# Adding x between two layers: accumulating transfers in place of loads and GpSimd adds

## The chip, the cores and the metric

The kernel runs on one core of one Trainium2 chip. The metric is the device time of one execution in microseconds (us). Three executions of the kernel before took 1881.49, 1882.27 and 1885.61 us, so the median is 1882.27 us. A further execution was profiled; all rows below are from it.

## The reference

A two-layer encoder trunk in float32, for 16 meta tokens, 512 prompt frames and 32 sample frames (560 columns in all), each with 2048 features:

```
def layer_forward(x, ...):
    u = rms_norm(x, pre_g)
    proj = einsum('btd,dc->btc', u, w_in)       # 2048 -> 6144 columns
    ...                                          # RG-LRU branch ya, attention branch yb
    y = einsum('btc,cd->btd', concatenate([ya, yb], -1), w_out)
    x = x + rms_norm(y, post_g)                  # <- the step that the change is about
    return x, ...
for l in range(2): x = layer_forward(x, ...)
```

The addition `x + rms_norm(y, post_g)` stands twice: between the layers, where the sum feeds layer 1 (`g_post` in the kernel), and at the end, where it is the output (`g_last`).

## The kernel before

Everything is held with features on the 128 partitions and the 560 columns along the free axis, so each activation is 16 feature tiles of 128x560. Weights and activations are float32, split into a high and a low part (`whi`, `wlo`; `uhi`, `ulo`); a product is three TensorE matmuls of 280 columns (`mm3`, L293 on, the matmul is L301): high x high, low activation x high weight, high activation x low weight. Weights come in chunks of 256 KB, four 128x128 blocks: SyncE loads `raw` (four buffers, L251), ScalarE rounds it to `whi` (L271) up to three chunks ahead of use (`w_ahead`), VectorE subtracts to get `wlo` (L281).

`R` holds 16 tiles of 128x560: first the mixed branches, then the rows of `y`. x itself does not fit in SBUF beside them; it lies in DRAM (`XD`).

Order is written by hand. All work beside the matmul stream is in Python generators that the class `Side` steps: after every two `mm3` (six matmuls, one tick) up to two generators that are due advance by one step, and `yield n` puts the next step n ticks on. Every engine takes its own instructions in this order, and waits for data that is not there.

Around the change: the last six output tiles of layer 0's W_out are computed for columns 0 to 279 (half 0), then again for columns 280 to 559 (half 1), each tile from four chunks. After each output tile `ev_y` scales it out of PSUM into `R` (VectorE, L1193), squares it (ScalarE, L1196) and sums the squares in `xcp` (GpSimd, L1200). At the end of half 0 the generator `0post0` is started (`side.add`, L1243), so it runs beside half 1's matmuls; `0post1` waits for it and runs beside layer 1's first products (`rows`, L1129), which for each feature tile k first ask that `ulo[k]` has been issued (`st["ready"]`).

One `g_post` (L991) makes the reciprocal root of the mean square (`rstd_half`, 128x280 matmul with ones at L428, Ln and Exp on ScalarE, four VectorE steps), then runs 19 steps. Step s multiplies `R[s]` by it (VectorE, L1015), adds x (GpSimd, L1016) from a buffer that a ScalarE-queued transfer filled one step earlier (L1001); two steps later ScalarE rounds the sum times the gain to `uhi` (L1020), stores the new x to DRAM (L1021) and squares it (L350); VectorE on every fourth tile, GpSimd on the others, adds the squares in the tile `accx` (L353, named e in the profile); one step later VectorE makes `ulo` (L1025). The pauses after the steps are 2, 2 and 4 ticks in turn (`RP`).

Of the kernel before, what the change touches and what calls it, by code (L numbers as in the profile page):

```python
# [10 lines left out]
F32 = mybir.dt.float32  # L11
F32R = mybir.dt.float32r
ACTF = mybir.ActivationFunctionType
ALU = mybir.AluOpType
# [13 lines left out]
T = META + SEQ + DEC  # L28
S0 = META + SEQ
KT = 16  # L30
# [7 lines left out]
WRAW, WSP = 4, 4  # L38

NB = 6  # L40
RP = (2, 2, 4)

KEPT = (("KH1", "KH2"), ("KL", "Q1"), ("Q2", "xch"), ("xcl", "Vh"), ("Vl", "MS"), ("PTh",), ("PTl",))
DQ, DS, DL = 7, 8, 9
# [1 line left out]
LY = 9  # L46
LF = 7
XR = 1
KF = 6
KRD, KPD, VRD, QPD = 6, 3, 2, 1  # L50
LS, L1, HL = 9, 1, 3
# [59 lines left out]
def hymba_step(ctx, tc, ins, onehot, outs):  # L111
    nc = tc.nc
    side = Side()
    st = {"of": [], "c": [0], "s": [0, 0], "c_i": 0, "s_i": 0}
# [11 lines left out]
    big = ctx.enter_context(tc.tile_pool(name="big", bufs=1))  # L126
# [3 lines left out]
    dram = ctx.enter_context(tc.tile_pool(name="dram", bufs=1, space=DRAM))  # L130
# [24 lines left out]

    uhi = [big.tile([128, T], F32R, name=f"uhi{k}") for k in range(KT)]
    ulo = [big.tile([128, T], F32R, name=f"ulo{k}") for k in range(KT)]
    R = [big.tile([128, T], F32, name=f"R{k}") for k in range(KT)]
    rstd = big.tile([128, T], F32, name="rstd")
    XD = [dram.tile([128, T], F32, name=f"xd{k}") for k in range(KT)]  # L160

    act_set(NLE)
    ident = const.tile([128, 128], F32, name="ident")
# [14 lines left out]
    def load_x(c):  # L178
        for i in range(4):
            nc.sync.dma_start(out=R[4 * c + i][:, 0:512],  # L180
                              in_=ins["x_prompt"][0, 128 * i:128 * i + 128, 512 * c:512 * c + 512])
# [37 lines left out]
    for l in range(DEPTH):  # L219
# [8 lines left out]
        for m in range(2, KT - NB):  # L228
            chunks += col_chunks(w_out, m)
            k = m - 3  # L230
# [130 lines left out]
    def x_squares(n):  # L361
# [3 lines left out]
        acc = ssq[:, 4 * i + c:4 * i + c + 1]  # L365
        x = R[min(4 * c + i, 15)][:, 0:512]
        if i < 4 and i % 2:
# [8 lines left out]
    def x_first(k):  # L376
# [5 lines left out]
        for i in range(4):  # L382
            p, at = (pa, META + 128 * i) if i < 2 else (pb, 128 * i - 256)
            nc.tensor.transpose(p[:, at:at + 128], R[4 * c + i][:, cs] if k else x0[:, i, :], ident)
        nc.tensor.transpose(pa[:, 0:META], v[DEC:DEC + META, ms], ident[DEC:DEC + META, DEC:DEC + META])
# [182 lines left out]
    def k_end(l, h):  # L568
# [4 lines left out]
        nc.gpsimd.tensor_copy(out=KS[:, PAST:PAST + DEC], in_=kT[:, S0:T])  # L573
        cK = R[8 + h][:, 0:512].rearrange("p (j c) -> p j c", j=4)
        cV = tmp.tile([128, 4, 128], F32, tag="cV", name="cV")
# [134 lines left out]
    def g_att(l, h, c0):  # L710
# [4 lines left out]
        PTs = tmp.tile([128, 5, 32], F32, tag="PTs", name="PTs")  # L715
        ot = R[8 + h]
        sq = wide("sq")
# [268 lines left out]
    def x_buffers():  # L986
        a, b = wide("i"), wide("r")
        c, d = (tmp.tile([128, n], F32, tag=t, name="xr") for t, n in (("KS", PAST + DEC), ("cV", 512)))
        return [a[:, 0:288], c, b[:, 0:288], d, a[:, 288:576], BM[:, 64:528], b[:, 288:576]]

    def g_post(l, half, ssy, ry):  # L991
        lo, hi = halves(l)[half]
        cs = slice(lo, hi)
        if not half:
            st["xr"] = x_buffers()
        xr = {}

        def load(k):
            if k < KT:
                xr[k] = st["xr"][k % 7][:, 0:hi - lo]  # L1000
                nc.scalar.dma_start(out=xr[k], in_=XD[k][:, cs])  # L1001

        while half and f"{l}post0" not in side.done:
            yield 1
        for k in range(XR):
            load(k)
        yield from grab("s", 5)
        rstd_half(ssy, ry, lo, hi, D)
        yield 2
        for s in range(KT + 3):  # L1010
            k = s
            if k < KT:
                r = R[k]
                load(k + XR)
                nc.vector.tensor_tensor(out=r[:, cs], in0=r[:, cs], in1=ry[:, cs], op=ALU.mult)  # L1015
                nc.gpsimd.tensor_tensor(out=r[:, cs], in0=r[:, cs], in1=xr[k], op=ALU.add)  # L1016
            k = s - 2
            if 0 <= k < KT:
                r = R[k]
                nc.scalar.activation(out=uhi[k][:, cs], in_=r[:, cs], func=ACTF.Copy, scale=col(l + 1, "pre", k))  # L1020
                nc.scalar.dma_start(out=XD[k][:, cs], in_=r[:, cs])  # L1021
                add_square(k, r[:, cs], lo, hi)
            k = s - 3
            if 0 <= k:
                nc.vector.scalar_tensor_tensor(out=ulo[k][:, cs], in0=R[k][:, cs], scalar=col(l + 1, "pre", k),  # L1025
                                               in1=uhi[k][:, cs].bitcast(F32), op0=ALU.mult, op1=ALU.subtract)
                st["ready"][half] = k + 1
            yield RP[s % len(RP)]
        yield from grab("s", 5)
        rstd_half([st["accx"][:, lo:hi]], rstd, lo, hi, D)  # L1030

# [3 lines left out]
    def x_late(k):  # L1035
# [3 lines left out]
        late[k] = late["t"][:, 288 * (k % 2):288 * (k % 2) + 288]  # L1039
        nc.sync.dma_start(out=late[k], in_=XD[k][:, 272:T])  # L1040

    def g_last(l, half, ssy, ry):
# [10 lines left out]

        for k in range(XR):
            load(k)
# [4 lines left out]
        for k in range(KT + 1 + lag):  # L1060
            if k < KT:
                load(k + XR)
                nc.vector.tensor_tensor(out=R[k][:, cs], in0=R[k][:, cs], in1=ry[:, cs], op=ALU.mult)  # L1063
# [25 lines left out]
    for l in range(DEPTH):  # L1089
# [38 lines left out]
        else:  # L1128
            def rows(half, acc, parts):  # L1129

                n = min(KF, len(KEPT))
                for part, ks in [(p, range(n)) for p in parts] + [(sum(parts, ()), range(n, KT))]:
# [25 lines left out]
        for kind, h in sched[l]:  # L1158
# [4 lines left out]
            for kc in range(4):  # L1163
                w = w_use()
                for kk in range(4):
                    k = 4 * kc + kk
# [17 lines left out]
        accy, ry = wide("xcp"), wide("sq")  # L1184
# [18 lines left out]
        for kc in range(8):  # L1203
            w = w_use()
            for kk in range(2):
                k = KT // 2 + 2 * kc + kk
# [84 lines left out]
```

## Time and profile before

| what | value |
|---|---|
| median of three executions | 1882.27 us (1881.49 to 1885.61) |
| the profiled execution | 1886.89 us |
| span of its instructions | 1885.2 us |
| TensorE matmul busy | 1843.5 us, 98% |
| VectorE busy | 1162.9 us, 62% |
| ScalarE busy | 909.5 us, 48% |
| GpSimd busy | 578.9 us, 31% |
| DMA, mean | 108 GB/s |

The engines are PE (TensorE matmuls), PEld (its weight loads), DVE (VectorE), ACT (ScalarE), POOL (GpSimd) and SP (SyncE); a name with q behind it is the engine's queue issuing a transfer. The half-0 tail of layer 0 ends at about 904.6 us of the span, half 1's matmuls run to about 951.6 us, and layer 1's first products from there to about 1007 us. A share of busy time over the whole span says little here: the place to read is the stretch from 904.6 to 1020 us.

### The profile page before, as it was taken

To read this page: it belongs to the slowest core of one execution; us is meant where nothing else is said; L and a number is where in the kernel's file an instruction comes from. 1 tells how busy PE (TensorE), PEld (TensorE's weight loads), DVE (VectorE), ACT (ScalarE), POOL (GpSimd) and SP (SyncE) were. 2 spreads that over 40 slices of the span, in tenths; PEclk is the share of its full clock that TensorE was granted. 3 is DMA by queue.
4 is the path that set the end of the run, shared out by engine and by line. 5 is a ranking of instruction groups with operands and counts; after the bars stand their busy time and mean duration, and the time that the engine had idled before them with its cause. 6 is when DMAs were issued, how large, how long until landed. Compare 5 with 4: busy or idle time off the path is not lost.

```text
span 1885.2 us, 37347 instructions
## 1 busy us (share of the span) xinstructions
PE 1843.5 (98%) x14196; PEld 1798.9 (95%) x14196; DVE 1162.9 (62%) x2484; ACT 909.5 (48%) x1831; POOL 578.9 (31%) x976
## 2 busy tenths in 40 slices
PE   7999999999999999999899999999999999999996
PEld 6999999999999999999888999999999999999995
DVE  6866656665666556434797776566565655563466
ACT  4555445454545536223555655453544544542343
POOL 3534232323323232011466242332423322211134
PEclk9999999999999999999999999999999999999998
DMA  7423232423333232335665232333323233233464
GB/s 232 130 77 105 76 104 65 110 75 109 83 89 99 74 111 71 99 100 142 197 196 150 60 111 75 107 94 87 107 76 108 64 110 100 78 93 115 125 192 140
DMA packets 334084, 204.35 MB, mean 108 GB/s; under 512 B 21100, under 2 KB 322612, under 8 KB 333904
## 3 DMA queue, kind: packets, MB, share of 16 engines
q1 hardware_dynamic: 311216, 164.44, 30.4%
q0 software_dynamic: 11168, 26.25, 5.0%
q10 hardware_dynamic: 11520, 11.28, 2.1%
q8 instruction: 111, 1.82, 0.4%
q14 instruction: 69, 0.57, 0.1%
HBM read 179.01 MB, written 22.89 MB: 107 GB/s over the span
## 4 chain that ended last, share of the span: by engine, by line
PE 87%; DVE 5%; issue 2%; POOL 2%; DMA 2%; ACT 1%; SPq 0%; ACTq 0%; DVEq 0%; POOLq 0%
PE pm L301 75%; PE sc L703 2%; PE sp L708 2%; DVE wlo L281 2%; PE sc L914 1%; PE sp L770 1%; PE sc L796 1%; PE sp L841 1%; PE sp L614 1%; DVE R L1063 1%; DMA raw<-in_w_in 1%; DMA R<-in_x_prompt 1%; DVE R L1015 0%; PE sc L301 0%; POOL R L1067 0%
## 5 line engine op out<-in xcount | busy, mean ns | idle before, releaser
L301 PE MATMUL pm<-uhi,whi 128*128 128x280 f32 (+3 forms) x3990 | 1181.9, 296 | 4.7 <-ACT whi L271 2.8
L301 PE MATMUL pm<-uhi,wlo 128*128 128x280 f32 (+3 forms) x3990 | 1160.5, 291 | 6.9 <-DVE wlo L281 6.8
L301 PE MATMUL pm<-ulo,whi 128*128 128x280 f32 (+3 forms) x3990 | 1158.8, 290 | 0.3 <-DVE ulo L395 0.3
L301 PEld LDWEIGHTS pm<-uhi,whi 128*128 128x128 f32 x3990 | 751.9, 188 | 18.1 <-issue 6.6
L301 PEld LDWEIGHTS pm<-uhi,wlo 128*128 128x128 f32 x3990 | 750.9, 188 | 10.7 <-DVE wlo L281 10.5
L301 PEld LDWEIGHTS pm<-ulo,whi 128*128 128x128 f32 x3990 | 752.2, 189 | 0.7 <-DVE ulo L395 0.6
L281 DVE TENSOR_TENSOR wlo<-raw,whi 128x512 fp32r<-128x512 f32 (+1 forms) x554 | 425.2, 774 | 264.5 <-ACT whi L271 261.2
L271 ACT CAST whi<-raw 128x512 fp32r<-128x512 f32 (+1 forms) x566 | 343.2, 614 | 388.8 <-PE pm L301 274.2
L689 ACT ACTIVATE e<-e,mx 128x144 f32<-128x144 f32 (+4 forms) x80 | 48.9, 611 | 165.5 <-DVE mx L686 165.5
L1200 POOL TENSOR_TENSOR xcp<-xcp,s 128x280 f32<-128x280 f32 (+2 forms) x56 | 43.1, 783 | 278.5 <-ACT s L1196 278.4
L140 ACT ACT_TABLE_LOAD x85 | 109.1, 1283 | 2.2 <-PEq L1273 0.8
L968 POOL TENSOR_TENSOR R<-R,z 128x280 f32<-128x280 f32 (+1 forms) x64 | 59.6, 954 | 147.1 <-DVE z L561 147.1
L761 POOL CAST PTm<-PTm 16x128 fp32r<-16x128 f32 (+1 forms) x72 | 22.0, 306 | 260.5 <-ACT PTm L756 260.2
L1196 ACT ACTIVATE s<-pm 128x280 f32<-128x280 f32 (+2 forms) x60 | 24.1, 402 | 125.3 <-DVE R L1193 124.6
L686 DVE CUSTOM_DVE_ANT_0 e<-sc,BM 128x144 f32<-128x144 f32 (+1 forms) x64 | 32.4, 507 | 57.6 <-PE sc L703 52.0
L844 DVE COPY R<-sp 128x288 f32<-128x288 f32 x16 | 7.3, 458 | 90.7 <-ACT sq L843 90.7
L1193 DVE TENSOR_SCALAR R<-pm,gvec 128x280 f32<-128x280 f32 (+2 forms) x64 | 30.2, 500 | 49.4 <-PE pm L301 49.4
L860 POOL TENSOR_TENSOR sq<-sq,s 128x560 f32<-128x560 f32 (+1 forms) x16 | 24.8, 1547 | 100.0 <-DVE s L444 96.2
L646 POOL COPY kv<-kv 128x16 f32<-128x16 f32 x15 | 3.0, 199 | 156.9 <-DVE kv L561 156.9
L703 PE MATMUL sc<-KH,Q 128*128 128x264 f32 (+4 forms) x176 | 45.2, 280 | 0.9 <-DVE mx L686 0.9
L703 PE MATMUL sc<-KL,Q 128*128 128x264 f32 (+4 forms) x176 | 45.3, 284 | 0.3 <-DVE KL L604 0.3
L689 ACT ACTIVATE s<-s,mx 128x144 f32<-128x144 f32 (+1 forms) x64 | 36.2, 565 | 19.6 <-DVE mx L686 17.8
(341 smaller groups left out, 2374.0 us busy)
## 6 DMA issues: line engine op xcount, KB each, us to landing
raw<-in_w_in SPq DMA_DIRECT2D x356, 256.0 KB, 2.9
raw<-in_w_out SPq DMA_DIRECT2D x176, 256.0 KB, 2.9
raw<-in_w_in SPq DMA_DIRECT2D x25, 192.0 KB, 3.3
xd<-R ACTq DMA_DIRECT2D x32, 140.0 KB, 2.8
R<-in_x_prompt SPq DMA_DIRECT2D x16, 256.0 KB, 5.2
R<-in_cache_k POOLq DMA_DIRECT2D x16, 256.0 KB, 4.9
cV<-in_cache_v POOLq DMA_DIRECT2D x16, 256.0 KB, 5.6
out_k_prompt<-s POOLq DMA_DIRECT2D x16, 256.0 KB, 5.2
```

The costliest lines, as they stand in the source:

```text
L140: nc.scalar.preload_act_table_set(name)
L271: nc.scalar.copy(out=hi[:, 0:n, :], in_=t[:, 0:n, :])
L281: q.tensor_tensor(out=lo[:, 0:n, :], in0=t[:, 0:n, :], in1=hi[:, 0:n, :].bitcast(F32), op=ALU.subtract)
L301: nc.tensor.matmul(out=ps[:, 0:n], lhsT=wt[:, blk, :], rhs=x[:, lo:hi], start=k == 0 and j == 0, stop=k == KT - 1 and j == 2)
L686: nc.vector.tensor_tensor_reduce(out=o2, in0=ps, in1=b2, scale=1.0, scalar=3.0e38, op0=ALU.add, op1=ALU.min, accum_out=m[0:rows, 0:1])
L689: nc.scalar.activation(out=o, in_=o, func=ACTF.Exp, scale=-1.0, bias=m[0:rows, 0:1], accum_out=m[0:rows, 1:2])
L703: nc.tensor.matmul(out=out, lhsT=st["Q"][m][:, qs], rhs=st[x][m][:, ks], start=x == "KH", stop=x == "KL")
L708: nc.tensor.matmul(out=out, lhsT=v[a], rhs=p[b], start=first and j == 0, stop=last and j == 2)
L860: nc.gpsimd.tensor_tensor(out=sq[:, c0:T], in0=sq[:, c0:T], in1=t[:, c0:T], op=ALU.mult)
L968: nc.gpsimd.tensor_tensor(out=r[:, lo:hi], in0=r[:, lo:hi], in1=z[:, lo:hi], op=ALU.mult)
L1193: nc.vector.tensor_scalar(out=R[m][:, cs], in0=ps[:, 0:hi - lo], scalar1=col(l, "post", m), scalar2=None, op0=ALU.mult)
L1200: nc.gpsimd.tensor_tensor(out=accy[:, cs], in0=accy[:, cs], in1=sq, op=ALU.add)
```

## The change

Between the layers x is added by the DMA engines. `R` and the DRAM copy of x become one tensor each (`RA`, `XA`), whose slices keep the old names, so that one transfer can span four feature tiles. After each fourth multiplication GpSimd issues one transfer that reads 128x4x280 values of x from DRAM and adds them into `RA` (`accum_op`). The loads into `xr` and the GpSimd additions of `g_post` are gone; `g_last` keeps its own. Steps now come every tick: multiplication s at step s, the transfer for tiles s-3 to s at s = 3, 7, 11, 15, `uhi` of tile k at step 12 + 2k, `ulo` at 14 + 2k; 45 steps in all.

```
+XB, XS, XL = 12, 2, 2
...
-    R = [big.tile([128, T], F32, name=f"R{k}") for k in range(KT)]
+    RA = big.tile([128, KT, T], F32, name="RA")
+    R = [RA[:, k, :] for k in range(KT)]
...
-    XD = [dram.tile([128, T], F32, name=f"xd{k}") for k in range(KT)]
+    XA = dram.tile([128, KT, T], F32, name="xa")
+    XD = [XA[:, k, :] for k in range(KT)]
...
-        for k in range(XR):
-            load(k)
         yield from grab("s", 5)
         rstd_half(ssy, ry, lo, hi, D)
         yield 2
-        for s in range(KT + 3):
-            k = s
-            if k < KT:
-                r = R[k]
-                load(k + XR)
-                nc.vector.tensor_tensor(out=r[:, cs], in0=r[:, cs], in1=ry[:, cs], op=ALU.mult)
-                nc.gpsimd.tensor_tensor(out=r[:, cs], in0=r[:, cs], in1=xr[k], op=ALU.add)
-            k = s - 2
-            if 0 <= k < KT:
+        for s in range(XB + XS * (KT - 1) + XL + 1):
+
+            if s < KT:
+                nc.vector.tensor_tensor(out=R[s][:, cs], in0=R[s][:, cs], in1=ry[:, cs], op=ALU.mult)
+                if s % 4 == 3:
+                    nc.gpsimd.dma_start(out=RA[:, s - 3:s + 1, cs], in_=XA[:, s - 3:s + 1, cs], accum_op=ALU.add)
+            k, o = divmod(s - XB, XS)
+            if 0 <= k < KT and o == 0:
                 r = R[k]
                 nc.scalar.activation(out=uhi[k][:, cs], in_=r[:, cs], func=ACTF.Copy, scale=col(l + 1, "pre", k))
                 nc.scalar.dma_start(out=XD[k][:, cs], in_=r[:, cs])
                 add_square(k, r[:, cs], lo, hi)
-            k = s - 3
-            if 0 <= k:
+            k, o = divmod(s - XB - XL, XS)
+            if 0 <= k < KT and o == 0:
                 nc.vector.scalar_tensor_tensor(out=ulo[k][:, cs], in0=R[k][:, cs], ...)
                 st["ready"][half] = k + 1
-            yield RP[s % len(RP)]
+            yield 1
```

GpSimd's queue where `0post0` starts, before (R_115 on are tiles 0 on of `R`; i, xr, r and BM are buffers of x; e is `accx`):

```order
L1016 TENSOR_TENSOR R_115<-R_115,i 128x280
L1200 TENSOR_TENSOR xcp<-xcp,s 128x280
L1016 TENSOR_TENSOR R_116<-R_116,xr 128x280
L1016 TENSOR_TENSOR R_117<-R_117,r 128x280
L1016 TENSOR_TENSOR R_118<-R_118,xr 128x280
L353 TENSOR_TENSOR e_9667<-e_9667,s 128x280
L1200 TENSOR_TENSOR xcp<-xcp,s 128x280
L1016 TENSOR_TENSOR R_119<-R_119,i 128x280
L353 TENSOR_TENSOR e_9667<-e_9667,s 128x280
L1016 TENSOR_TENSOR R_120<-R_120,BM 128x280
L1016 TENSOR_TENSOR R_121<-R_121,r 128x280
L353 TENSOR_TENSOR e_9667<-e_9667,s 128x280
```

The same place of GpSimd's queue now:

```order
L1007 DMA RA<-xa 128x4x280 x2
L1191 TENSOR_TENSOR xcp<-xcp,s 128x280
L1007 DMA RA<-xa 128x4x280
L356 TENSOR_TENSOR e_9637<-e_9637,s 128x280
L1007 DMA RA<-xa 128x4x280
L356 TENSOR_TENSOR e_9637<-e_9637,s 128x280
L1191 TENSOR_TENSOR xcp<-xcp,s 128x280
L356 TENSOR_TENSOR e_9637<-e_9637,s 128x280 x3
L1191 TENSOR_TENSOR xcp<-xcp,s 128x280
L356 TENSOR_TENSOR e_9637<-e_9637,s 128x280 x3
```

The additions of x have left the queue; four transfers stand in it, and the additions of squares stand closer together. ScalarE's queue up to the first `uhi` of half 0, before:

```order
L437 ACTIVATE sq<-sp,eps_t 128x280
L438 ACTIVATE sq<-sq 128x280
L271 CAST whi<-raw 128x512
L1001 DMA xr<-xd_133 128x280
L1196 ACTIVATE s<-pm 128x280
L271 CAST whi<-raw 128x512
L1001 DMA r<-xd_134 128x280
L271 CAST whi<-raw 128x512
L1001 DMA xr<-xd_135 128x280
L1020 ACTIVATE uhi_83<-R_115,gvec 128x280
L1021 DMA xd_132<-R_115 128x280
L350 ACTIVATE e_9667<-R_115 128x280
```

and now:

```order
L440 ACTIVATE sq<-sp,eps_t 128x280
L441 ACTIVATE sq<-sq 128x280
L274 CAST whi<-raw 128x512
L1187 ACTIVATE s<-pm 128x280
L274 CAST whi<-raw 128x512 x4
L1187 ACTIVATE s<-pm 128x280
L274 CAST whi<-raw 128x512 x2
L1011 ACTIVATE uhi_83<-RA,gvec 128x280
L1012 DMA xa<-RA 128x280
L353 ACTIVATE e_9637<-RA 128x280
L274 CAST whi<-raw 128x512
```

Four chunks' `whi` and one square of an output tile more stand ahead of the first `uhi`, and the issues of the loads are gone.

## Rows read from the trace of the kernel before

**Rows 1.** The page's head: the span, and busy time by engine.

```profile
span 1885.2 us, 37347 instructions
PE 1843.5 (98%) x14196; PEld 1798.9 (95%) x14196; DVE 1162.9 (62%) x2484; ACT 909.5 (48%) x1831; POOL 578.9 (31%) x976
```

**Rows 2.** Busy time by stretch; header names the columns, last row sums seven stretches.

```profile
core 0: us, PE busy (x) PEld busy (x) DVE busy (x) ACT busy (x) POOL busy (x), PEclk, DMA share, GB/s
...
904.60:913.70 9.10, 9.10 (x70) 8.91 (x69) 4.72 (x9) 4.88 (x8) 0.00 (x0) 1.00 0.60 170
913.70:951.60 37.90, 30.84 (x217) 28.11 (x215) 32.76 (x49) 20.51 (x48) 24.95 (x26) 1.00 0.74 212
...
978.50:1007.10 28.60, 26.02 (x191) 24.89 (x192) 27.00 (x41) 14.44 (x31) 21.35 (x26) 1.00 0.65 193
1007.10:1020.00 12.90, 11.67 (x92) 11.29 (x91) 11.01 (x21) 7.57 (x13) 8.50 (x13) 1.00 0.76 205
sum 124.70, PE 113.54 PEld 108.40 DVE 104.68 ACT 66.56 POOL 70.07; mean PE 16.22 PEld 15.49 DVE 14.95 ACT 9.51 POOL 10.01
```

**Rows 3.** Waits of PE, 913.7 to 951.6 us: total us, times, longest.

```profile
PE pm L301 <- DVE wlo L281: 4.9, 9, 1.1
PE pm L301 <- ACT whi L271: 1.5, 2, 1.2
```

**Rows 4.** Waits, 978.5 to 1020 us: PE's longest.

```profile
PE sc L301 <- DVE ulo L1025: 2.3, 3, 1.0
```

**Rows 5.** Groups by line and form, 913.7 to 951.6 us: busy us, mean ns.

```profile
L281 DVE TENSOR_TENSOR wlo<-raw,whi 128x512 fp32r<-128x512 f32 x18 | 18.8, 1061 | 5.1 <-ACT whi L271 5.1
...
L353 POOL TENSOR_TENSOR e<-e,s 128x280 f32<-128x280 f32 x8 | 8.5, 1066 | 0.0
L1015 DVE TENSOR_TENSOR R<-R,sq 128x280 f32<-128x280 f32 x14 | 8.5, 607 | 0.0
...
L1025 DVE SCALAR_TENSOR_TENSOR ulo<-R,gvec,uhi 128x280 fp32r<-128x280 f32 x10 | 6.0, 604 | 0.0
...
L1200 POOL TENSOR_TENSOR xcp<-xcp,s 128x280 f32<-128x280 f32 x5 | 3.9, 787 | 1.4 <-ACT s L1196 1.3
```

**Rows 6.** DVE in order of time: start, duration, instruction.

```profile
906.38 0.69 DVE L281 TENSOR_TENSOR wlo<-raw,whi 128x512 fp32r<-128x512 f32 x1 [1.04 <-ACT whi L271]
...
913.74 0.44 DVE L1015 TENSOR_TENSOR R<-R,sq 128x280 f32<-128x280 f32 x1
...
924.00 0.50 DVE L1025 SCALAR_TENSOR_TENSOR ulo<-R,gvec,uhi 128x280 fp32r<-128x280 f32 x1
924.42 1.28 DVE L281 TENSOR_TENSOR wlo<-raw,whi 128x512 fp32r<-128x512 f32 x1
...
1012.35 0.68 DVE L281 TENSOR_TENSOR wlo<-raw,whi 128x512 fp32r<-128x512 f32 x1
```

**Rows 7.** POOL in order of time, at two of those moments.

```profile
924.15 1.00 POOL L1016 TENSOR_TENSOR R<-R,i 128x280 f32<-128x280 f32 x1 [0.99 <-ACT uhi L1020]
...
1012.64 0.81 POOL L580 DMA_DIRECT2D R<-in_cache_k  x1
```

**Rows 8.** ACT in order of time, up to the first `uhi` of half 0.

```profile
914.70 0.41 ACT L1196 ACTIVATE s<-pm 128x280 f32<-128x280 f32 x1 [2.83 <-DVE R L1193]
...
916.03 0.53 ACT L1020 ACTIVATE uhi<-R,gvec 128x280 fp32r<-128x280 f32 x1
```

**Rows 9.** Busy time by stretch, 910 to 920 us (columns of rows 2).

```profile
910.00:920.00 10.00, 10.00 (x78) 9.95 (x77) 7.39 (x13) 5.52 (x12) 3.92 (x4) 1.00 0.64 177
```

**Rows 10.** DMA issues of the whole span: KB of one, median us to landing.

```profile
R<-in_cache_k POOLq DMA_DIRECT2D x16, 256.0 KB, 4.9
```

**Rows 11.** DMA queues, 904.6 to 951.6 us: packets, MB, share of 16 engines.

```profile
q1 hardware_dynamic: 11564, 5.72, 42.2%
q10 hardware_dynamic: 3847, 3.84, 28.6%
```

**Rows 12.** The chain that ended last: an unbroken run of matmuls.

```profile
878.70 30.71 PE pm L301 x238
```

More of the change, by code (lines that the diff above doesn't have):

```diff
@@ L40 @@
 NB = 6
-RP = (2, 2, 4)
 KEPT = (("KH1", "KH2"), ("KL", "Q1"), ("Q2", "xch"), ("xcl", "Vh"), ("Vl", "MS"), ("PTh",), ("PTl",))
@@ L993, in g_post @@
         cs = slice(lo, hi)
[L994 to L998, printed above, removed]
-            if k < KT:
-                xr[k] = st["xr"][k % 7][:, 0:hi - lo]
-                nc.scalar.dma_start(out=xr[k], in_=XD[k][:, cs])
         while half and f"{l}post0" not in side.done:
             yield 1
-        for k in range(XR):
-            load(k)
         yield from grab("s", 5)
@@ L1009, in g_post @@
         yield 2
-        for s in range(KT + 3):
-            k = s
-            if k < KT:
-                r = R[k]
-                load(k + XR)
-                nc.vector.tensor_tensor(out=r[:, cs], in0=r[:, cs], in1=ry[:, cs], op=ALU.mult)
-                nc.gpsimd.tensor_tensor(out=r[:, cs], in0=r[:, cs], in1=xr[k], op=ALU.add)
-            k = s - 2
-            if 0 <= k < KT:
+        for s in range(XB + XS * (KT - 1) + XL + 1):
[5 more added lines that the diff above has]
+            if 0 <= k < KT and o == 0:
                 r = R[k]
```

## The prediction, written before the changed kernel ran

> **What bounds the kernel now.** I read the page's head first [rows 1]: the matmul engine is busy 98% of the span. So no edit beside the matmul stream can gain more than the matmul stream now loses where that edit works. The second view, busy time by stretch, says how much that is [rows 2]. Seven stretches from the last evacuation before `0post0` to the end of the layer change last 124.7 us, of which matmuls run 113.54, so 11.2 us are lost. The reader is to see where they lie: 7.06 us between 913.7 and 951.6 (37.90 less 30.84), where `0post0` runs; 2.58 between 978.5 and 1007.1, where `0post1` runs; 1.23 behind it. In the first of these, the waits say why [rows 3]: 4.9 us for `wlo` from VectorE, 1.5 for `whi` from ScalarE. In the second, 2.3 us for `ulo` from VectorE [rows 4]. VectorE sets the pace in both.
>
> VectorE is slow there and not only loaded. Alone, `wlo` takes 0.69 us, the multiplication 0.44 and `ulo` 0.50; while a GpSimd addition runs, `wlo` takes 1.28 [rows 6, 7]. In the stretch their means are 1.061, 0.607 and 0.604 us [rows 5]. The excess over the lone times is 18 x 0.37 + 14 x 0.167 + 10 x 0.104 = 6.7 + 2.3 + 1.0 = 10.0 us. GpSimd does 26 instructions there [rows 2], 8 sums of squares and 5 additions into `xcp` [rows 5], so the other 13 are the additions of x.
>
> **The change part by part.** *Removed: 32 additions of x on GpSimd.* In the stretch of `0post0` 13 of 26 go, so I let half of VectorE's excess go, 5.0 us, and matmuls lose 7.06 - 5.0 = 2.1 instead of 7.1: **-5.0 us**. Bounds: -2.5, if the remaining additions of squares, now two ticks apart and not 2.67, hit VectorE more often; -7.1, if the stall goes whole. The multiplications do not go away, they come forward, one a tick. Two chunks' worth of ticks then hold 2 `wlo` and 4 multiplications, 2 x 0.69 + 4 x 0.44 = 3.1 us, in eight `mm3`. From an unbroken run, 238 matmuls in 30.71 us [rows 12], a matmul takes 0.129 us, a tick of six 0.774, a chunk of twelve 1.55; two chunks are 3.1 us. So VectorE is just full for the first 16 ticks, and lighter after.
>
> *Removed: 32 load issues on ScalarE, and their landings.* ScalarE is busy 20.5 of 37.9 us [rows 2]; I cost it at nothing.
>
> *Added: eight transfers, four to a half, and a wait for each.* The place that decides is ScalarE's queue at the first `uhi` of half 0, since the `whi` of the next chunks are queued behind it and matmuls wait for those. That `uhi` ran at 916.03 [rows 8], 4 ticks after step 0 (pauses 2 and 2); now it stands 12 ticks after, 8 x 0.774 = 6.2 us later, at 922.2. The transfer is issued when the fourth multiplication is done. The first started at 913.74 [rows 6]; up to the fourth's end stand four multiplications, one evacuation of about 0.5 and one `wlo`: 4 x 0.44 + 0.5 + 0.69 = 2.95, so 916.7, or 917.7 where `wlo` first waits 1.04 as in rows 6. I take 917.0, which leaves 5.2 us. No row shows an accumulating transfer. The nearest is GpSimd's load of 256 KB with as many rows (128x4), 4.9 us from issue to landing [rows 10]. One transfer here has 128 x 4 x 280 x 4 = 573,440 bytes, 560 KB. Rate: SyncE's queue moved 5.72 MB in 42.2% of 47.0 us [rows 11], 288 GB/s with all engines busy. Low bound: 4.9 us, if size and adding cost nothing. High: 4.9 x 560/256 = 10.7. My value: 4.9 + 304 KB more (1.1 us) + a second pass over the bytes for the read of what is added to (2.0 us) = 8.0, nearer to the row of the load. ScalarE then waits 8.0 - 5.2 = 2.8 us. That much is covered: ScalarE waited 2.83 us at 914.70 [rows 8] and matmuls were busy 10.00 of 10 us there [rows 9], since `whi` is made up to three chunks (4.6 us) ahead. I charge **+1.0 us** for what VectorE can't catch up; bounds 0, and 10.7 - 5.2 - 2.8 = 2.7.
> The Trainium skill, "DMA: Bandwidth & Descriptors" (Anatomy of one DMA), fits a GpSimd-issued transfer as 2.0 us plus its bytes at 436 GB/s. By that this one would take an estimated 3.3 us, land ahead of its `uhi`, and the sum below would be a microsecond better. But the same fit gives 2.6 us for the load that the trace has at 4.9, so the measurement decides.
>
> The issue itself takes GpSimd 0.81 us, and `wlo` beside one took 0.68, its lone time [rows 6, 7]; eight issues replace 32 additions, and cost nothing. Behind each waiting issue on GpSimd stand sums into `xcp`; ScalarE's squares need their buffers, three of them, which covers a wait of two or three microseconds.
>
> *DMA engines.* In 47.0 us the queues of SyncE and ScalarE used 42.2% + 28.6% of the engines, 33.3 us of full work [rows 11]. Without the stall that stretch is 39.9 us long (47.0 - 7.06). If a byte that is added costs double, 16 tiles of 143,360 bytes more at 288 GB/s are 8.0 us: 41.3 us of work, 1.4 too much. I charge **+0.5**; bounds 0 and 1.4.
>
> *`0post1`.* The same relief for `ulo` against 2.58 us lost [rows 2, 4]: **-1.5**, bounds 0 and -2.6. Its first `uhi` has 9 ticks for the transfer too, while layer 1's first products use weights that are already split, so I charge no wait.
>
> *Steps.* A half took 19 steps with 50 ticks of pauses and now takes 45; two halves end 10 ticks, 7.7 us, sooner. The 1.23 us behind `0post1` [rows 2] contain the wait for its root: **-1.0**, bounds 0 and -1.2.
>
> Sum: -5.0 + 1.0 + 0.5 - 1.5 - 1.0 = **-6.0 us**, from the profiled execution's 1886.89 to 1880.9. That execution lies 4.6 us above the median; against the median of 1882.27 it is **1876.3**. The forecast's own range is 1871.5 (nearly all 11.2 us back) to 1880.
>
> **The rivals.**
> *Contention stays.* The sums of squares, 12 of 16 on GpSimd in each half, come in 32 ticks instead of 43, so they meet VectorE more often: the first term is -2.5, `0post1` gains nothing, and -2.5 + 1.0 + 0.5 - 1.0 = -2.0, **1880.3**. For it: a sum of squares holds GpSimd 1.066 us on average [rows 5], as long as an addition of x. Against: VectorE then has nothing but `wlo`, `ulo` and a quarter of the sums.
>
> *The transfers arrive too slowly; slower.* Place: ScalarE at `uhi` of tiles 4, 8 and 12. These come four tiles, 8 ticks, 6.2 us apart; above 6.2 us from landing to landing each of the three waits. Price: weights take 256 KB per 1.55 us, 169 of 288 GB/s, 59%. A group at double cost is 4.0 us of all engines; in the other 41% it takes 9.8. So 3 x (9.8 - 6.2) = 10.8, and the first landing at the high bound 2.7 where I had 1.0; with the other terms, -6.0 + 10.8 + 1.7 = +6.5, **1888.8**. For it: DMA engines are busy 0.74 there already [rows 2]. Against: the total of 41.3 us above fits into the stretch, and a transfer that waits can also take its turn from the weights, four buffers of which are loaded ahead.
> The Trainium skill's same page (Issuing engines are not separate DMA queues) speaks for this rival: transfers from all engines run on the same 16 DMA engines, so work taken off GpSimd is not free there. The trace has no row of two queues slowing each other at full load.
>
> *The whole stall goes.* Landings stay within the 5.2 us, and VectorE with its multiplications done early never falls behind: -7.1 - 2.6 - 1.2 = -10.9, **1871.4**. Against: GpSimd still does half its work there.
>
> *The change does nothing, or more waits appear than written.* With all tiles of `R` in one tensor a transfer for half 0 could hold up half 1's evacuations. Their columns are disjoint, and such a wait would put evacuations behind landings; I give it little and count it with the slow case.
>
> **How the numbers follow.** A measurement of this kernel can tell about 0.2%, 3.8 us, from no change: faster is below 1878.5, slower above 1886.0. Chances: forecast 0.52 (faster 0.43, same 0.09), contention stays 0.21 (0.05 faster, 0.14 same, 0.02 slower), slow transfers 0.19 (0.18 slower, 0.01 same), whole stall gone 0.08. Faster 0.56, same 0.24, slower 0.20. The range goes from 1871 to 1888, and leaves out about half of the slow case.
>
> **What would show it.** In the changed profile: `wlo` nearer to 0.7 than to 1.06 us beside `0post0`; transfers `RA<-xa` landing in about 8 us; a wait of some 3 us on ScalarE ahead of the first `uhi`, with matmuls still busy, and none ahead of the fifth; matmul loss from 904.6 to 1020 us near 5 us. If landings are over 12 us or ScalarE waits ahead of the fifth, ninth and thirteenth `uhi`, the prediction is wrong on the slow side; if `wlo` stays above 1 us with GpSimd's additions gone, its first term is.

## The result, and the profile after

The changed kernel takes 1893.14 us (median of six executions, 1890.25 to 1896.29), the kernel before 1882.68 us beside it. The ratio is 1.0053 (95% interval 1.0043 to 1.0063): slower by about 10 us, where I had forecast 6 us faster. The profiled execution took 1893.49 us. Lines below the change have moved: the matmul is L304, `whi` L274, `wlo` L284, the multiplication L1005, the adding transfer L1007, `uhi` L1011, the store L1012, `ulo` L1016.

Two of my predictions can be read off at once. VectorE's groups from 913.7 to 951.6 us, to hold against [rows 5]:

```profile
L284 DVE TENSOR_TENSOR wlo<-raw,whi 128x512 fp32r<-128x512 f32 x17 | 13.4, 790 | 12.7 <-ACT whi L274 12.6
L1016 DVE SCALAR_TENSOR_TENSOR ulo<-RA,gvec,uhi 128x280 fp32r<-128x280 f32 x10 | 7.2, 716 | 0.0
L1005 DVE TENSOR_TENSOR RA<-RA,sq 128x280 f32<-128x280 f32 x14 | 5.7, 438 | 0.0
```

`wlo` fell from 1061 to 790 ns, the multiplication from 607 to 438, while `ulo` rose from 604 to 716: VectorE is relieved. But it now idles 12.7 us ahead of `wlo`, waiting for `whi`. ScalarE's queue around the first `uhi` of half 0 (in brackets the idle time before an instruction and what ended it), against [rows 8]:

```profile
922.83 0.53 ACT L1011 ACTIVATE uhi<-RA,gvec 128x280 fp32r<-128x280 f32 x1 [2.91 <-DMA RA<-xa]
...
926.38 0.62 ACT L274 CAST whi<-raw 128x512 fp32r<-128x512 f32 x1 [1.39 <-DMA raw<-in_w_out]
...
931.30 0.62 ACT L274 CAST whi<-raw 128x512 fp32r<-128x512 f32 x1 [2.24 <-DMA raw<-in_w_out]
```

The wait for the transfer is 2.91 us; I had 2.8. The rows under it matter more: ScalarE waits for weights, 9.5 us for `whi` from 904 to 1020 us where it was 2.3 before. The DMA queues and issues from 917 to 940 us (packets, MB, share of the 16 engines; KB of one, median us to landing) say why:

```profile
q0 software_dynamic: 2112, 2.29, 62.7%
q1 hardware_dynamic: 4399, 2.18, 37.2%
q10 hardware_dynamic: 981, 0.98, 12.2%
...
raw<-in_w_out SPq DMA_DIRECT2D x8, 256.0 KB, 9.6
RA<-xa POOLq DMA_DIRECT2D x3, 560.0 KB, 10.6
```

The same view of the kernel before:

```profile
q1 hardware_dynamic: 5959, 2.96, 44.7%
q10 hardware_dynamic: 2265, 2.25, 33.8%
...
raw<-in_w_out SPq DMA_DIRECT2D x11, 256.0 KB, 3.4
```

The adding transfers (q0) take 62.7% of the engines in 23 us. The shares sum to 112% where 78.5% were before. (A share is the time that packets took, and packets can overlap, so the sum can pass 100%, as here; I read that as full engines.) Weights want 44.7%, if the rate of before is what they need, and get 37.2%; a load that landed after 3.4 us lands after 9.6, and four buffers of 256 KB hold only four chunks of 1.55 us, 6.2 us of matmuls. The matmul engine's waits from 904 to 1020 us (total, times, longest) have changed hands from VectorE [rows 3, 4] to `whi`:

```profile
PE pm L304 <- ACT whi L274: 6.7, 7, 2.6
PE sc L304 <- DVE ulo L1016: 3.5, 2, 2.4
PE sp L431 <- DVE e L356: 2.3, 1, 2.3
PE pm L304 <- DVE wlo L284: 2.1, 8, 0.4
```

The chain that ended last runs through these loads (start, us):

```profile
914.74 8.07 DMA RA<-xa
923.61 0.63 ACT whi L274
924.26 0.70 DVE wlo L284
924.98 12.65 DMA raw<-in_w_out
...
970.57 7.32 DMA raw<-in_w_in
977.91 11.64 DMA raw<-in_w_in
```

The first row is my transfer, 8.07 us where I had 8.0. The three long ones behind it are weights. And a second loss follows the first, in the stretches around a wait for `whi` (columns of [rows 2]):

```profile
926.00:929.00 3.00, 2.32 (x16) 1.87 (x15) 2.16 (x5) 1.72 (x4) 2.08 (x2) 1.00 1.16 243
929.00:932.00 3.00, 0.35 (x4) 0.13 (x2) 0.05 (x1) 0.76 (x3) 0.79 (x2) 1.00 1.17 267
932.00:936.00 4.00, 3.30 (x13) 2.74 (x13) 1.63 (x4) 1.45 (x4) 0.00 (x0) 0.57 1.18 216
936.00:940.00 4.00, 4.00 (x18) 3.77 (x19) 2.49 (x5) 2.90 (x8) 1.72 (x2) 0.58 0.97 298
```

Matmuls stop for 2.6 us, up to 932; behind that the granted clock is 0.57 and 0.58, mostly the lower of its two levels (1.2 GHz instead of 2.4). Two of its matmuls show the pace:

```profile
934.27 0.43 PE L304 MATMUL pm<-uhi,wlo 128*128 128x280 f32 x1
934.50 0.43 PE L304 MATMUL pm<-uhi,whi 128*128 128x280 f32 x1
```

They start 0.23 us apart; 0.129 was normal [rows 12]. "Busy" hides this: the engine is busy 4.00 of 4 us and issues 18 matmuls.

A cleaner measure of the section alone is the time from the first matmul of `0post0`'s root to layer 1's first score matmul. After:

```profile
906.44 0.63 PE L431 MATMUL sp<-xcp,ones 128*128 128x280 f32 x2
...
1025.81 0.23 PE L706 MATMUL sc<-KH,Q 128*128 128x144 f32 x1
```

Before:

```profile
909.25 0.63 PE L428 MATMUL sp<-xcp,ones 128*128 128x280 f32 x2
...
1019.79 0.23 PE L703 MATMUL sc<-KH,Q 128*128 128x144 f32 x1
```

That is 119.37 us after and 110.54 before, 8.8 more. The medians differ by 10.5 us, and these two executions by 6.6, since the changed one was 2.8 us earlier at the root. The two sections as stretches, after and then before (columns of [rows 2]):

```profile
906.44:1025.81 119.37, 104.85 (x726) 99.45 (x725) 82.04 (x151) 59.74 (x128) 43.49 (x55) 0.94 0.75 181
909.25:1019.79 110.54, 99.38 (x727) 94.24 (x725) 96.73 (x151) 59.67 (x128) 69.07 (x79) 1.00 0.69 196
```

They hold the same matmuls (726 and 727 on record). These are busy 5.5 us longer, at a mean granted clock of 0.94 instead of 1.00; the other 3.4 of the 8.8 us is idle time.

### The profile page after: what moved, and what is told of

Read it like the earlier page. It is cut to its first block, busy times and chain, and to the rows that moved or that the text cites. A ratio compares the mean times of both kernels' runs of the same rounds, so it can differ in the third digit from the quotient of the medians.

```text
span 1891.8 us, 37271 instructions
## 1 busy us (share of the span) xinstructions
PE 1847.6 (98%) x14196; PEld 1801.8 (95%) x14196; DVE 1149.5 (61%) x2484; ACT 909.6 (48%) x1831; POOL 551.4 (29%) x952
## 4 chain that ended last, share of the span: by engine, by line
PE 85%; DVE 5%; DMA 4%; issue 3%; ACT 2%; POOL 2%; SPq 0%; ACTq 0%; POOLq 0%; DVEq 0%
PE pm L304 73%; PE sc L706 2%; PE sp L711 2%; DMA raw<-in_w_in 2%; PE sc L917 1%; DVE wlo L284 1%; DMA raw<-in_w_out 1%; PE sp L773 1%; PE sc L799 1%; DVE RA L1054 1%; PE sp L617 1%; PE sc L304 1%; PE sp L844 1%; DMA RA<-in_x_prompt 0%; DMA RA<-xa 0%
## 5 line engine op out<-in xcount | busy, mean ns | idle before, releaser
L304 PE MATMUL pm<-uhi,whi 128*128 128x280 f32 (+3 forms) x3990 | 1184.0, 297 | 10.0 <-ACT whi L274 8.1
L304 PE MATMUL pm<-uhi,wlo 128*128 128x280 f32 (+3 forms) x3990 | 1161.6, 291 | 2.9 <-DVE wlo L284 2.9
L304 PE MATMUL pm<-ulo,whi 128*128 128x280 f32 (+3 forms) x3990 | 1159.8, 291 | 0.2 <-DVE ulo L398 0.2
L304 PEld LDWEIGHTS pm<-uhi,whi 128*128 128x128 f32 x3990 | 753.0, 189 | 24.9 <-ACT whi L274 10.1
L304 PEld LDWEIGHTS pm<-uhi,wlo 128*128 128x128 f32 x3990 | 751.6, 188 | 6.3 <-DVE wlo L284 5.9
L304 PEld LDWEIGHTS pm<-ulo,whi 128*128 128x128 f32 x3990 | 753.0, 189 | 0.7 <-DVE ulo L398 0.6
L284 DVE TENSOR_TENSOR wlo<-raw,whi 128x512 fp32r<-128x512 f32 (+1 forms) x554 | 416.9, 758 | 285.3 <-ACT whi L274 281.6
L274 ACT CAST whi<-raw 128x512 fp32r<-128x512 f32 (+1 forms) x566 | 344.0, 614 | 411.8 <-PE pm L304 289.6
L971 POOL TENSOR_TENSOR RA<-RA,z 128x280 f32<-128x280 f32 (+1 forms) x64 | 59.6, 952 | 147.1 <-DVE z L564 147.1
L847 DVE COPY RA<-sp 128x288 f32<-128x288 f32 x16 | 7.3, 458 | 90.6 <-ACT sq L846 90.6
L1184 DVE TENSOR_SCALAR RA<-pm,gvec 128x280 f32<-128x280 f32 (+2 forms) x64 | 30.2, 501 | 49.1 <-PE pm L304 49.1
## 6 DMA issues: line engine op xcount, KB each, us to landing
RA<-xa POOLq DMA_DIRECT2D x8, 560.0 KB, 10.2
```

The lines of the kernel that those rows point to most:

```text
L274: nc.scalar.copy(out=hi[:, 0:n, :], in_=t[:, 0:n, :])
L284: q.tensor_tensor(out=lo[:, 0:n, :], in0=t[:, 0:n, :], in1=hi[:, 0:n, :].bitcast(F32), op=ALU.subtract)
L304: nc.tensor.matmul(out=ps[:, 0:n], lhsT=wt[:, blk, :], rhs=x[:, lo:hi], start=k == 0 and j == 0, stop=k == KT - 1 and j == 2)
L971: nc.gpsimd.tensor_tensor(out=r[:, lo:hi], in0=r[:, lo:hi], in1=z[:, lo:hi], op=ALU.mult)
L1184: nc.vector.tensor_scalar(out=R[m][:, cs], in0=ps[:, 0:hi - lo], scalar1=col(l, "post", m), scalar2=None, op0=ALU.mult)
```

## The experiments

The theory of crowding says: the transfers take engine time from the weight loads, `whi` comes late, matmuls stop, and the clock falls. Its rivals are ScalarE's wait at the first `uhi`, the new order of steps, and ScalarE's stores. In the table, the section is the measure just shown, as its difference from 110.54 us. It comes from one profiled execution, so it can differ from the median by some us.

| run | median us | ratio to before (95%) | section |
|---|---|---|---|
| changed kernel | 1893.14 | 1.0053 (1.0043 to 1.0063) | +8.8 |
| no transfers | 1876.55 | 0.9957 (0.9945 to 0.9969) | -6.4 |
| plain copies | 1879.39 | 0.9976 (0.9966 to 0.9986) | -6.7 |
| first `uhi` later | 1894.57 | 1.0058 (1.0042 to 1.0074) | +13.1 |
| spread | 1884.81 | 1.0011 (1.0002 to 1.0021) | +5.5 |
| pairs | 1882.37 | 0.9998 (0.9990 to 1.0007) | +1.5 |
| half 0 alone | 1885.84 | 1.0015 (1.0006 to 1.0024) | +3.5 |
| half 1 alone | 1888.16 | 1.0024 (1.0016 to 1.0033) | +3.5 |
| half 1 alone, long runs | 1886.60 | 1.0017 (1.0008 to 1.0026) | +1.3 |
| stores by GpSimd | 1893.17 | 1.0065 (1.0051 to 1.0078) | +10.2 |
| half 0 paced | 1888.77 | 1.0029 (1.0018 to 1.0039) | +5.5 |
| every other tile | 1890.44 | 1.0039 (1.0025 to 1.0054) | +5.9 |
| half 0 paced, half 1 as before | 1889.20 | 1.0038 (1.0025 to 1.0050) | +7.3 |
| half 0 every other, half 1 as before | 1890.01 | 1.0039 (1.0027 to 1.0052) | +3.9 |
| half 0 by single tiles, half 1 as before | 1887.90 | 1.0028 (1.0017 to 1.0040) | +5.6 |
| half 1 in pairs, half 0 as before | 1883.50 | 1.0006 (0.9995 to 1.0016) | +0.6 |
| mixed | 1887.72 | 1.0024 (1.0015 to 1.0033) | +4.9 |
| half 0 mixed, half 1 in pairs | 1884.95 | 1.0014 (1.0005 to 1.0023) | -0.1 |

**No transfers.**

```
-                if s % 4 == 3:
-                    nc.gpsimd.dma_start(out=RA[...], in_=XA[...], accum_op=ALU.add)
```

> The changed kernel without its eight accumulating transfers: x is not added between the layers, all else (steps, packing of R and x, stores) stays. Crowding theory (the transfers take the DMA engines from the weight loads, whi comes late, matmuls stop and the granted clock falls): the whole loss goes and VectorE's relief stays, 1872 to 1880 us, with raw landings back at 3.3 us median and below 6 at most. Order theory (multiplications all in the first 16 ticks, or R as one tensor, are what costs): stays at 1890 us or more. Wait theory (ScalarE stands still at the first uhi of each half): also 1872 to 1880, told apart by the run with the later first uhi.

1876.55 us, 7.1 below the kernel before (1883.62 in that set). The run leaves x out between the layers. The loss goes whole and the relief stays; raw landings are at most 5.0 us (13.4 in the changed kernel). The order of steps and the packing of `R` are not the cause. The rows of 913.7 to 951.6 us, against 217 matmuls in [rows 2]:

```profile
913.70:951.60 37.90, 32.43 (x229) 29.82 (x229) 32.83 (x55) 22.50 (x53) 13.70 (x15) 1.00 0.68 200
```

**Plain copies.**

```
-  nc.gpsimd.dma_start(out=RA[...], in_=XA[...], accum_op=ALU.add)
+  nc.gpsimd.dma_start(out=RA[...], in_=XA[...])
```

> The changed kernel with the eight transfers as plain copies: x overwrites the scaled rows instead of being added to them; bytes written, issue places and waits stay. If adding is what makes the transfers long (159 GB/s against 288 for plain loads): transfers land in 5 to 7 us, engine time of the queue about 8 us instead of 14.4, and the kernel takes 1876 to 1886 us. If it is the bytes alone, bunched as they are: landings near 9 us, 1889 us or more.

1879.39 us: of the transfers' cost, 16.6 us between the changed kernel and the run without transfers, the plain bytes are 2.8 by the medians (the sections show no cost), and no instruction waits for these copies. The rest is the adding, with the waits that its longer landings bring. The queue and issues of the copies from 917 to 940 us:

```profile
q0 software_dynamic: 576, 2.29, 31.0%
...
RA<-xa POOLq DMA_DIRECT2D x4, 560.0 KB, 6.6
```

The same 2.29 MB took 31.0% of 23 us, 7.1 us of all engines, where the adding took 62.7%, 14.4 us.

**First `uhi` later.**

```
-XB, XS, XL = 12, 2, 2
+XB, XS, XL = 18, 2, 2
```

> The changed kernel with the first uhi of each half 6 ticks (4.6 us) later, nothing else: the transfers stay bunched, and ScalarE's waits of 2.9 and 1.9 us for them go. Wait theory: the loss goes with the waits, 1878 to 1884 us. Crowding theory: weights still land late behind the bunch, so at most 3 us come back, 1890 to 1894 us, and matmuls still run at half clock behind a gap near 930 us.

1894.57 us. No instruction waits for the transfers any more, and nothing came back. But the later `uhi` brings a wait of its own in half 1. The matmul engine's waits from 904 to 1020 us:

```profile
PE pm L304 <- ACT whi L274: 7.7, 6, 1.7
...
PE sc L304 <- ACT uhi L1011: 5.8, 1, 5.8
```

So the time alone doesn't price ScalarE's wait. What does speak is the first line: the waits for `whi` stay (6.7 us in the changed kernel, 7.7 here) with ScalarE's wait gone. That wait, the one danger that I had priced, is not what makes the weights late. My expectation of half clock near 930 us missed: there are four waits of 1.5 to 1.8 us for `whi` there and the granted clock is 1.00; it falls to 0.50 with the wait of 5.8 us.

**Spread, and pairs.** Spread has a transfer of four tiles every 8 ticks and its first `uhi` at step 18; pairs has two tiles every 4 ticks and `uhi` where the changed kernel has it. Both:

```
-            if s < KT:
-                nc.vector.tensor_tensor(out=R[s]..., in0=R[s]..., in1=ry...)
-                if s % 4 == 3:    # RA[:, s - 3:s + 1, cs]
+            k, o = divmod(s, 2)
+            if k < KT and o == 0:
+                nc.vector.tensor_tensor(out=R[k]..., in0=R[k]..., in1=ry...)
+                if k % 4 == 3:    # spread: RA[:, k - 3:k + 1, cs]
+                if k % 2:         # pairs:  RA[:, k - 1:k + 1, cs]
```

> The changed kernel with one multiplication every second tick, so a transfer every 8 ticks (6.2 us) instead of every 4 (3.1 us), and the first uhi at step 18 instead of 12. Crowding theory: the four transfers of a half then have 25 us instead of 12, weights keep more of the engines, half or more of the loss goes: 1880 to 1887 us, raw landings at most 8 us. Wait theory: like the run that only starts uhi later. Order theory (front-loaded multiplications): also below 1887, but then with raw landings unchanged.

> The changed kernel in both halves with a multiplication every second tick and a transfer of two tiles every 4 ticks; uhi, ulo and the 45 ticks as in the changed kernel. Only the bunch is taken apart: the same bytes leave over 25 us instead of 12. Crowding theory: half or more of the 16.6 us above the run without transfers comes back, 1880 to 1886 us, and ScalarE waits under 2 us for a first uhi. Bytes alone (engine time of 14 us per half whatever the pacing): 1889 us or more.

1884.81 and 1882.37 us. The same bytes, added in the same way, cost 8 to 11 us less when half 0's transfers are issued over 26 us (spread) or 30 us (pairs) instead of 12. The first `uhi` of the spread run is six ticks later, and its matmuls wait 2.4 us for `uhi` and 3.6 for `ulo`, against none and 1.0 in pairs. (The section of the spread run, +5.5, is one execution and says more than its median, +1.2; why they differ is open.) In the run in pairs, the queues from 917 to 940 us:

```profile
q0 software_dynamic: 1528, 1.62, 49.4%
q1 hardware_dynamic: 5338, 2.65, 41.0%
q10 hardware_dynamic: 1008, 1.00, 12.5%
...
raw<-in_w_out SPq DMA_DIRECT2D x9, 256.0 KB, 5.5
```

Weights land in 5.5 us instead of 9.6. The engines are still full (103%), which is why it only equals the kernel before. ScalarE still waits 4.4 us ahead of `uhi` for the transfers, in three waits of up to 2.6 (my expectation said under 2 for a first `uhi`), nearly the 4.8 of the changed kernel, and the loss against the kernel before is gone all the same.

**Half 0 alone, half 1 alone.** The other half loads x and adds it on GpSimd as before.

```
-  (g_post if l < DEPTH - 1 else g_last)
+  ((g_post, g_post_add)[b] if l < DEPTH - 1 else g_last)    # and the reverse
```

> Accumulating transfers for half 0 alone; half 1 loads x and adds it on GpSimd with the pauses 2, 2, 4 as in the kernel before. Crowding theory: half 0 has all weight chunks to fetch beside the transfers, so most of the loss is there: 1886 to 1892 us. If each half costs the same, 1888 us. If half 1 alone is the bad place (its late first products), 1878 to 1882 us.

> Accumulating transfers for half 1 alone; half 0 loads x and adds it on GpSimd as in the kernel before. If each half costs the same, 1888 us; with the crowding worst beside half 0, 1883 to 1887 us; if half 1 alone is the bad place, 1892 us or more. The differences of this run and of the one with half 0 alone from the kernel before should add to the 10.5 us of both, if the halves do not act on each other.

+2.6 and +4.9 us against 1883.22 in that set: 7.5 of the 10.5. Both halves lose; I had expected most of it in half 0, and the medians say half 1 (the sections say equal shares). In half 1 the late weights hold up ScalarE's queue: with half 1 alone its squares wait up to 2.8 us for weights, matmuls wait 5.8 us in one place for `ulo`, and the chain that ended last has a long load of weights just there (a wait; start and us of the load):

```profile
PE sc L305 <- DVE ulo L1017: 6.1, 2, 5.8
...
967.95 11.80 DMA raw<-in_w_in
```

What the remaining 3 us are stays open.

**Long runs.** Half 1 alone, with other shapes:

```
-  RA[:, s - 3:s + 1, cs]
+  RA[:, s - 3:s - 1, :]
```

> The run with half 1 alone (1888.2 us), its four transfers reshaped: two whole tiles of 560 columns each instead of four of 280, so the same 560 KB lie in runs of 4480 bytes to a partition instead of 1120. It leaves half of half 1's tiles without x, and adds x twice to columns 0 to 279 of the others. If an accumulating transfer is priced by its runs (2112 packets in half 0's stretch of the changed kernel, at 0.11 us of one engine each): the queue's share halves, landings 5 to 7 us, 1881 to 1885 us. If by its bytes (a read of the target beside the write): landings stay at 8 to 12 us and the time within 2 us of 1888.

Between the two: landings are 7.1 us in the middle instead of 9.9. The medians are 1.6 us apart, but the intervals of the two ratios overlap, so a gain in time is not shown. (The run leaves x out of half of half 1's tiles.) The queue from 960 to 1007 us took 26.2% in 576 packets; with half 1 alone and short runs it took 30.9% in 2112:

```profile
q0 software_dynamic: 576, 2.29, 26.2%
```

That is 12.3 us of all engines against 14.5. So of the 7 us of engine time that adding costs over plain copies (7.1 us), the short runs carry 2; the other 5 stay at the same 576 packets.

**Stores by GpSimd.** `nc.scalar.dma_start(out=XD[k]...)` becomes `nc.gpsimd.dma_start`.

> The changed kernel with the 32 stores of the new x issued from GpSimd instead of ScalarE; transfers stay bunched. In the changed kernel ScalarE stood still for 8.4 us behind stores that waited for late weight loads. If those stalls carry the loss (they delay whi and uhi behind them): 1882 to 1888 us. Crowding theory without that relay (late weight loads alone carry it): 1889 to 1895 us.

1893.17 us, no better. In the changed kernel ScalarE's squares stood 8.4 us behind stores that waited for weights, here 0.9, but that relay does not carry the loss.

**Half 0 taken apart, half 1 left.** Five runs pace half 0 in different ways; their edits are new step tables:

```
half 0 paced:      multiplication at 5 * k // 2, uhi at 18 + 5 * k // 2
every other tile:  the kernel before, odd tiles by nc.gpsimd.dma_start(out=R[k], in_=XD[k], accum_op=ALU.add),
                   uhi two steps later, in both halves
half 1 as before:  g_post_add for half 1, half 0 paced, every other tile, or all 16 single tiles
```

> The changed kernel with half 0 paced wider: a multiplication every 2.5 ticks, so a transfer every 10 ticks (7.7 us), the first uhi at step 18 and one every 2.5 ticks; half 1 as in the changed kernel. Crowding theory: the loss of half 0 goes nearly whole, that of half 1 stays: 1882 to 1887 us. If spreading half 0 only moves its stores and transfers into half 1's time, 1888 us or more.

> The kernel before, with x added to the odd tiles by accumulating transfers of one tile each (16 of 140 KB) and to the even tiles by load and GpSimd as before; pauses 2, 2, 4 stay, uhi two steps later. Crowding theory: half the accumulated bytes, spread over 33 us of a half instead of 12, leave room for the weights, and half of VectorE's relief (3.5 of 7.1 us) comes through: 1877 to 1882 us, raw landings at most 7 us. If any accumulating transfer beside the weights costs (by its own bytes, however spread): 1885 us or more.

> Half 0 with accumulating transfers of four tiles, one every 10 ticks, as in the paced run; half 1 loads x and adds it on GpSimd as before. In the paced run half 0's stretch of 37.9 us held 255 matmuls against 217 before, and the loss came in half 1. Crowding theory: half 0's gain stays once half 1 has no transfers, 1877 to 1881 us. If the later end of half 0 only pushes half 1 back: 1883 us or more.

> Half 0 with x added to odd tiles by transfers of one tile and to even tiles by load and GpSimd; half 1 as before. In the run with both halves so, half 0's stretch held 247 matmuls against 217, and the loss came in half 1, whose ulo is two steps later. Crowding theory: 1878 to 1881 us. If the transfers cost by their bytes however spread: 1884 us or more.

> Half 0 with x added to all 16 tiles by transfers of one tile each, at the steps of the kernel before (2, 2 and 4 ticks apart), uhi two steps later; half 1 as before. Same bytes as in the run with half 0 alone (1885.8 us), in 33 us instead of 12 and in pieces of 140 KB. Crowding theory: raw landings at most 7 us and 1877 to 1882 us. If the bytes alone count: 1885 us or more.

All are 1887.9 to 1890.4 us. All are above what the theory of crowding gave in my expectations, the first by 2 us, the others by 6 to 9. Half 0 did get better: with every other tile and half 1 as before, its stretch holds 245 matmuls against 217, and raw landings are at most 5.3 us. The gain is lost in half 1, where the waits of the matmul engine from 904 to 1020 us are:

```profile
PE sc L301 <- DVE ulo L1069: 6.6, 6, 2.5
PE pm L301 <- DVE wlo L281: 2.8, 3, 1.6
PE sp L614 <- DVE z L561: 2.4, 1, 2.4
```

In [rows 4] `ulo` was 2.3. These versions give half 0 6 to 8 ticks more than the kernel before; `0post1` waits for its end, starts its root about as long after that of `0post0` as before (52.8 us, 52.3 before) although the matmuls are some 30 further on, and layer 1 catches up with its `ulo`. So the time for the transfers can't simply be lengthened; that this lateness is the whole of their loss is argued from the waits and not tested.

**Half 1 in pairs; mixed.** Half 1 in pairs leaves half 0 as before. Mixed gives odd tiles single transfers and even tiles loads with GpSimd additions, at the steps of the run in pairs with `uhi` from step 10. The last run has this in half 0 and pairs in half 1.

```
+                if k % 2 == 0:
+                    nc.gpsimd.tensor_tensor(out=R[k]..., in0=R[k]..., in1=xr.pop(k), op=ALU.add)
+                elif k % 2:
+                    nc.gpsimd.dma_start(out=R[k]..., in_=XD[k]..., accum_op=ALU.add)
```

> Half 1 alone by accumulating transfers, paced: a multiplication every second tick, a transfer of two tiles (280 KB) every 4 ticks (3.1 us), uhi at the same steps as in the changed kernel, 45 ticks in all; half 0 loads and adds as before. Crowding theory: half 1 needs only ten chunks of weights in 25 us, so paced transfers leave them room: 1879 to 1884 us, raw landings at most 8 us. If half 1 loses by its late ulo and not by the weights: 1886 us or more.

> Meant to beat both: steps of the run in pairs (a multiplication every second tick), but x goes to the odd tiles by a transfer of one tile and to the even tiles by load and GpSimd, uhi from step 10, 43 ticks to a half against 50 in the kernel before. Accumulated bytes are halved (about 7 us of all DMA engines to a half, and 3.6 for the loads), half of VectorE's relief stays. Crowding theory: 1876 to 1881 us, raw landings at most 6 us. If GpSimd with its additions, sums and issues can't keep 1.55 us to a tile: 1884 us or more, with ulo late.

> Half 0 as in the mixed run (odd tiles by transfers of one tile, even tiles by load and GpSimd, uhi from step 10), half 1 by paced transfers of two tiles with uhi from step 12. Half 1 fetches weights less often, so the accumulated bytes fit there: 1876 to 1881 us. If half 1's transfers still cost: as the run with half 1 paced alone, 1883 us.

1883.50, 1887.72 and 1884.95 us. Half 1 in pairs costs nothing that can be measured. The mixed run, meant to win, loses: landings are short (raw at most 5.6 us), but with GpSimd adding again VectorE is slow again. Its multiplications from 913.7 to 951.6 us:

```profile
L1015 DVE TENSOR_TENSOR RA<-RA,sq 128x280 f32<-128x280 f32 x15 | 12.7, 848 | 0.0
```

848 ns against 438 in the changed kernel. What the matmuls wait for is `whi` (6.0 us in that stretch) although weights land in time; that the slow VectorE delays it through ScalarE's queue is argued, not shown. None of the versions that add x beats the kernel before.

## Why the prediction was wrong

**VectorE's relief, `0post1` and the steps** (-5.0, -1.5, -1.0, together -7.5): right in sum, since the run without transfers measures -7.1, but partly by luck. By the matmul waits from 904 to 1020 us, those for `wlo` and `whi` fall from 7.3 to 3.2 us in that run (-4.1 where I had -5.0) and those for `ulo` from 2.3 to nothing (-2.3 where I had -1.5). The term for the steps rests on a misreading: the 1.23 us behind `0post1` were no wait for its root, but one wait of a later matmul for VectorE's `z`:

```profile
PE sp L614 <- DVE z L561: 1.2, 1, 1.2
```

It goes too. Against that stands a wait that I had not foreseen: with the new steps the root at the end of `0post0` waits 2.3 us for its last sum of squares, with transfers or without.

**The first landing** (8.0 us, a wait of 2.8, charged +1.0): the landing was 8.07 and the wait 2.91. So near a hit is partly luck: all eight transfers landed in 6.9 to 11.4 us, 10.2 in the middle. That the wait is not the loss fits the runs: without it matmuls still waited 7.7 us for `whi`, and in pairs ScalarE waited 4.4 us with the loss against the kernel before gone. Its own price is not shown.

**The issue** (0.81 us on GpSimd, at nothing): it took 1.28 to 1.39 us. No run shows a price; GpSimd is busy 15.57 of 37.9 us there, where it was 24.95.

**DMA engines (+0.5, bounds 0 and 1.4): this is the step that failed.** With the first landing's +1.0 I had the transfers at +1.5; they cost 16.6 (1893.14 less 1876.55). The matmul loss from 904.6 to 1020 us, which I had put near 5 us, is 14.5. The work itself was sized well: I had 16.0 us of all engines to a half, the rows give 14.4. What was wrong is the stretch to which I held it. I compared 41.3 us of work with a stretch of 39.9 and charged a third of the overhang. But multiplications a tick apart issued half 0's four transfers in 12 us. From 917 to 940 us the engines were asked for 62.7% (transfers), 44.7% (weights at the rate of before) and 12.2% (stores), 120% together, and a queue of weights has slack for 6.2 us, not for 9.6. Plain copies at half the price fit and cost 2.8; the same bytes in pairs cost 11 us less. The transfers do not slow VectorE itself: its multiplication takes 438 ns with them and 437 without.

**Half 1's weights, at nothing.** I charged no wait in `0post1`, because layer 1's first products use weights that are already split. The weights that follow them crowd just as well: half 1 alone cost 4.9 us, and its matmuls waited 5.8 us for an `ulo` while one load of weights took 11.80 us.

The Trainium skill, "Collectives: The Full Stack" (The bandwidth ceiling: the fold count and why AG ≠ RS ≠ AR), says of the adding step of a collective, ReduceScatter, that not the add costs but its second source read, so that it runs at about half the rate of AllGather's copy. The factor is the same here, 14.4 us against 7.1, though with long runs it is 12.3; that the second read is the reason no run shows. The Trainium skill, "DMA: Bandwidth & Descriptors" (Issuing engines are not separate DMA queues), says that transfers from all engines share 16 DMA engines; when I weighed it no row showed two queues slowing each other. Now one does: weights issued by SyncE go from 3.4 to 9.6 us when GpSimd's transfers run.

**The clock**: not in the prediction at all; [rows 2] gave 1.00 in every stretch. In the changed kernel it fell to 0.57 behind a wait of 2.6 us, and over the section 5.5 of the 8.8 us are longer busy time and not gaps. When a wait brings this on, these runs don't settle. The root's wait for its last sum of squares was 2.31 us without transfers and 2.35 with plain copies; behind it (first line without transfers, second with plain copies; columns of [rows 2])

```profile
952.00:956.00 4.00, 4.00 (x17) 3.48 (x16) 1.94 (x6) 2.03 (x5) 0.00 (x0) 0.58 0.00 0
957.20:961.20 4.00, 4.00 (x26) 3.72 (x27) 2.88 (x8) 2.37 (x5) 0.00 (x0) 1.00 0.00 0
```

the clock fell in one run and not in the other. In pairs it fell to 0.57 behind waits of at most 1.4 us. So what a gap costs beyond its own length can be read here only afterwards.

**The rival "the transfers arrive too slowly"** had the right resource and the right side (1888.8), at the wrong place. I had it at the fifth, ninth and thirteenth `uhi`. Those never waited: only the first of each half did. The transfers took their turn from the weights, as I wrote there, but as an argument against a loss; it was the loss.

**Contention stays, the whole stall goes, waits that are not written**: `wlo` at 790 ns speaks against the first, the result against the second. Of the third nothing shows; `uhi` is the only instruction between 904 and 1020 us that waits for a transfer of x.

## What to carry to other kernels

Work that moves from an engine to DMA is paid from the 16 engines, here at double for an addition, and it must be held against what streams through them in the very stretch between issue and landing, not in the whole stage: sum the queue shares over those microseconds, and over 100% ask who waits in line and how much is loaded ahead of it. Where a matmul stream is the bound, a gap can cost more than its own length, so look at the granted clock beside busy time, and compare stretches that hold the same matmuls.

## What the runs showed of the hardware

- An accumulating transfer into SBUF, beside weight loads, moved 159 GB/s with all engines (2.29 MB in 14.4 us), a plain copy of the same tiles 322 (7.1 us). In runs of 4480 bytes it was 186 (12.3 us). Full engines are not the reason: for single tiles, with every other tile and half 1 as before, 0.72 MB took 22.6% of 23 us, 139 GB/s, where all queues together took 97%.
- For the same tiles the plain copy made 576 packets, the accumulating one 2112; GpSimd's issue took 0.76 us for the copy and 1.29 for the accumulating transfer.
- Behind a wait of 2.6 us the granted clock fell to 0.57 and matmuls started 0.23 instead of 0.129 us apart until 939. Of two waits of 2.3 us at the same place, one was followed by a lower clock and one was not.
- The time to the first matmul of `0post0`'s root, before the steps that these kernels change, lay between 902 and 911 us in their profiled executions. That is why differences of 5 us need the section or several executions.
